# Gates and two projections of a hybrid decoder layer: weights as the moving operand, and a merged matrix turned by transposes

## The chip, the core and the metric

The kernel runs on one core of one Trainium2 chip. The metric is the device time of one execution in microseconds (us), the median of several runs. A core has a matrix engine (TensorE, PE), a vector engine (VectorE, DVE), a scalar engine (ScalarE, ACT), GpSimd (POOL), a sync engine (SyncE, SP) that here only issues transfers, and 16 DMA engines. Each engine works through its own instructions in order; semaphores connect them.

## The reference

One decoder layer over 256 tokens of width 2048, float32. Two mixers share one normalised input and one input projection; their outputs are projected, weighted by gates, added, projected again and added to the input:

```python
h = rms_norm(x, norm_w)
p = h @ w_in                                   # 2048 x 12416
(p_r, p_k, p_v, z_a, p_wd, p_ad, p_q, p_kq, p_vq, z_b, g_a, g_b) = split(p)
y_a = rwkv7_mix(p_r, p_k, p_v, p_wd, p_ad, ...) * silu(z_a)      # 16 heads of 64, recurrence
y_b = moba_attention(p_q, p_kq, p_vq, ...) * silu(z_b)           # 16 heads of 64, causal
merged = sigmoid(g_a) * (y_a @ w_proj_rwkv) + sigmoid(g_b) * (y_b @ w_proj_moba)
x = x + merged @ w_out
```

With 256 tokens the attention has one block, so it is plain causal attention. `g_a` and `g_b` are 2048 columns each; both projections go from 1024 to 2048 columns.

## The kernel before

**Three passes for one product.** Every large product is done in a reduced float32 format (fp32r) with both operands split into a high and a low part: hi x hi, lo x hi and hi x lo are added up in PSUM. The normalised input, turned so that channels lie in partitions, stands split in `xh` and `xl`. The row scale of the normalisation is not in them; it is applied to results, as `rbc` (tokens along columns) or `rsx` (tokens in partitions).

**Weights.** A chunk is 512 columns of a weight matrix. Its rows come in loads of 1 MB (`emit_load`, L235, two buffers `raw`), issued by SP. Each load makes two half-loads ("jobs" in the code) of 128 partitions x 1024 numbers: four blocks of 128 rows for a load, two for a half-load. ACT copies a half-load rounded into `hi` (L216), DVE subtracts to get `lo` (L222); three buffers each. A half-load is split two ahead of its use. There are 258 half-loads: 98 for the first seven projections of both head groups, 32 for the two SiLU gates, 64 for the sigmoid gates, 32 for the two projections, 32 for the output projection. In the rest of this text they are counted from 0.

**Two forms of the product.** `mm_fm` (L329) has 128 weight columns stationary and 256 tokens moving; the result has channels in partitions. One half-load is 2 row blocks x 4 column blocks x 3 = 24 passes of 256 columns. `mm_tm` (L347 to L349) has 128 tokens stationary and 512 weight columns moving; the result has tokens in partitions. One half-load is 2 row blocks x 2 token blocks x 3 = 12 passes of 512 columns. Before the change the attention's q, k and v and the output projection use `mm_tm`, all else `mm_fm`.

**Side work.** The recurrence (`rwkv_elem`, `rwkv_r`, `rwkv_mid`, `rwkv_v`, `group_norm`) and the attention (`moba`) are generators. After each half-load `pump` takes one step of the queue and one of each urgent generator. In `moba`, L831 makes logits, L842 to L845 mask them and take the maximum, L849 is the exp, L856 and L857 normalise, L863 and L865 turn the probabilities, L878 multiplies by v. `rwkv_v` and `group_norm` use L672, L679, L696, L699, L706, L734, L743, L750, L753.

**Gates and projections.** `gate_post` scales a gate chunk by `rbc` on DVE (`normed`, L170) into slots of old buffers and takes the sigmoid on ACT (L930). ACT keeps the tables of one set of functions at a time: sigmoid, exp and root lie in different sets, and a change shows as ACT_TABLE_LOAD. `pb_post` multiplies the attention's projection by its gate, `pa_post` the recurrence's, adds both, and splits the sum into `mgh` and `mgl`, the stationary operands of the output projection.

**Order.** For all but the first six half-loads the order within each engine is made by a scheduler, which runs a model of the engines over the whole program. So an edit at one place can move instructions that it doesn't touch.

Of the kernel before, what the change touches and what calls it, by code (L numbers as in the profile page):

```python
# [36 lines left out]
def tile_hybrid_block(ctx: ExitStack, tc: tile.TileContext, x, pv, wdu, wau,  # L37
# [23 lines left out]
    def PSS():  # L61
        return psd.tile([P, 512], F32, tag="ps", name=nm("ps"))
# [4 lines left out]
    def f32(ap):  # L67
        return ap.bitcast(F32)
# [100 lines left out]
    def normed(o, ps):  # L169
        dve.tensor_tensor(o.rearrange("p (f t) -> p f t", f=2), ps.rearrange("p (f t) -> p f t", f=2),  # L170
                          rbc2, ALU.mult)
# [68 lines left out]
    def chunk(wsrc, c0, w, kts, mm, post, pre=None, acc=None):  # L240
        nk = 2048 // w
        st = {}
        for b in range(kts // nk):
            ld = dict(spec=(wsrc, b * nk * P, nk, c0, w))
            loads.append(ld)
            for hf in range(2):
                jobs.append(dict(ld=len(loads) - 1, hf=hf, st=st, mm=mm, k0=b * nk + hf * nk // 2,
                                 nk=nk // 2, w=w, last=kts - 1, first=(b == 0 and hf == 0),
                                 end=(b == kts // nk - 1 and hf == 1), post=post, pre=pre))
# [84 lines left out]
    def mm_tm(sh, sl, cuts=((0, 0, 512), (1, 0, 512)), done=None):  # L334
        def f(jb):
            st, w, nk = jb["st"], jb["w"], jb["nk"]
            if jb["first"]:
                st["ps"] = [PSS() if i > 1 else PSM() for i in range(len(cuts))]
            hi = jb["hi"].rearrange("p (k c) -> p k c", k=nk)
            lo = jb["lo"].rearrange("p (k c) -> p k c", k=nk)  # L340
            order = [(i, q) for i in range(nk) for q in range(len(cuts))]
            for i, q in sorted(order, key=lambda e: e[1]) if jb is jobs[-1] else order:
                t, ca, cb = cuts[q]
                k = jb["k0"] + i
                o = st["ps"][q][:, 0:cb - ca]
                ts, cs, end = slice(t * P, (t + 1) * P), slice(ca, cb), k == jb["last"]
                pe.matmul(o, sh[:, k, ts], hi[:, i, cs], start=(k == 0), stop=False)  # L347
                pe.matmul(o, sh[:, k, ts], lo[:, i, cs], start=False, stop=False)  # L348
                pe.matmul(o, sl[:, k, ts], hi[:, i, cs], start=False, stop=end)  # L349
                if end and done:  # L350
                    done(o, t, ca, cb)
        return f

    fm_x = mm_fm(lambda k: xh[:, k, :], lambda k: xl[:, k, :])
    tm_x = mm_tm(xh, xl)

    R = [dict(), dict()]
    wa = C("wa", [P, S])
# [562 lines left out]
    def gate_post(key, i):  # L921
        def post(st):
            if not gates:
                for tag, n in (("LL0", 4), ("LL1", 4), ("X64", 2), ("UV", 4), ("a", 2)):
                    gt = T(tag, [P, n, 512])
                    gslots.extend(gt[:, u, :] for u in range(n))
            for j in range(2):
                gt = gslots.pop(0)
                normed(gt, st["ps"][j])
                act.activation(gt, gt, AF.Sigmoid)  # L930
                gates[key, 2 * i + j] = gt
        return post

    ysp = {}
# [30 lines left out]
            dve.tensor_tensor(lv, y, f32(hv), ALU.subtract)  # L965
            yield

    def fm_y(key):
        return mm_fm(lambda k: ysp[key, "h"][k // 4][:, k % 4, :],
                     lambda k: ysp[key, "l"][k // 4][:, k % 4, :])  # L970

    mrg = {}
# [9 lines left out]

    mh_t, ml_t = [], []

    def pa_post(i):
        def post(st):
            if not mh_t:
                mh_t.append(cp.tile([P, KT, S], F32R, tag="xh", name="mgh"))
                ml_t.append(cp.tile([P, KT, S], F32R, tag="xl", name="mgl"))
            mt = T(("cs", "kk")[i % 2], [P, 2, 512])  # L990
            for j in range(2):
                m = mt[:, j, :]
                dve.tensor_tensor(m, gates["a", 2 * i + j], st["ps"][j], ALU.mult)
                dve.tensor_tensor(m, m, mrg[i, j], ALU.add)
                f0 = 4 * i + 2 * j
                hv = mh_t[0][:, f0:f0 + 2, :].rearrange("p f t -> p (f t)")
                lv = ml_t[0][:, f0:f0 + 2, :].rearrange("p f t -> p (f t)")
                act.activation(hv, m, AF.Copy)
                dve.tensor_tensor(lv, m, f32(hv), ALU.subtract)
        return post  # L1000

    def out_pre(i, st_x):
# [14 lines left out]
        return done  # L1017

    def out_mm(cuts, done):
        return lambda jb: mm_tm(mh_t[0], ml_t[0], cuts, done)(jb)  # L1020

    def then(post, *gens):
        def f(st):
# [5 lines left out]
    def need(mark):  # L1029
        return lambda: drain(mark)  # L1030
# [28 lines left out]
        chunk(w_in, C_ZA + 512 * i, 512, KT, fm_x, post)  # L1059
    for ki, key in enumerate("ab"):  # L1060
        for i in range(4):
            chunk(w_in, (C_GA if key == "a" else C_GB) + 512 * i, 512, KT, fm_x,
                  with_need("v1", gate_post(key, i)))
    for i in range(4):
        chunk(w_pm, 512 * i, 512, 8, fm_y("b"), pb_post(i), pre=need("y"))
        chunk(w_pr, 512 * i, 512, 8, fm_y("a"), pa_post(i))
    for i in range(4):
        sx = {}
        cuts = ((0, 0, 512), (1, 0, 256), (1, 256, 512)) if i == 3 else ((0, 0, 512), (1, 0, 512))
# [46 lines left out]
```

## Time and profile before

| | |
|---|---|
| median of 3 runs | 831.94 us (830.06 to 832.64) |
| the profiled execution | 834.34 us |
| its span, first to last instruction | 832.6 us |
| PE, PE weight loads, DVE, ACT, POOL busy | 98%, 92%, 66%, 50%, 4% |
| moved by DMA | 145.78 MB, 175 GB/s |
| two sigmoid gates and both projections, without side work | 519.80 to 740.67 us |
| output projection | 740.67 us to the end |

PE is the engine to look at: at 98% there is little time in which it waits. Matmuls are pipelined, so the duration of one (0.28 us for 256 columns) is longer than the distance from its start to the next one's start; in the timeline the distance is what counts, and it is called the pitch or the pace below. The same holds, to a lesser degree, of ACT and DVE: a row that begins before the last one's end shows the overlap. A row with "x8" stands for eight instructions that follow each other; a small float32 matmul appears as two instructions.

### The profile page before, as it was taken

How to read it: one execution, taken by the hardware profiler on the slowest of the kernel's cores; microseconds unless marked ns; L12 is line 12 of the kernel's file. 1: busy time of each engine (PE TensorE's matmuls, PEld its weight loads, DVE VectorE, ACT ScalarE, POOL GpSimd, SP SyncE). 2: the span in 40 equal slices, each digit the busy share in tenths (PEclk: the TensorE clock that was granted, in tenths of full speed). 3: DMA queues.
4: the chain of work that ended last, by engine and by line, in shares of the span. 5: the costliest groups of instructions: out<-in, count | busy, mean ns of one | idle time of the engine just before them, and what ended most of it. 6: DMA issues, size and time to landing. Idle time of an engine off the chain costs nothing.

```text
span 832.6 us, 15909 instructions
## 1 busy us (share of the span) xinstructions
PE 819.9 (98%) x6770; PEld 764.4 (92%) x6770; DVE 551.9 (66%) x776; ACT 417.8 (50%) x565; POOL 29.9 (4%) x42
## 2 busy tenths in 40 slices
PE   8999999999999999999999999999999999999998
PEld 7999778899998888999999999999999999998887
DVE  5869958956569679649974588644445566665453
ACT  6785446444437784444444487444344444443332
POOL 5001100000000003000000000000000000000000
PEclk9999999999999999999999999999999999999999
DMA  8564554654434544655673424655555555556772
GB/s 305 181 201 152 180 166 160 202 177 153 136 119 131 174 146 137 210 140 178 203 228 106 149 66 143 224 189 172 198 194 169 195 193 166 199 182 202 248 232 97
DMA packets 83206, 145.78 MB, mean 175 GB/s; under 512 B 11568, under 2 KB 13872, under 8 KB 83136
## 3 DMA queue, kind: packets, MB, share of 16 engines
q1 hardware_dynamic: 71584, 138.55, 51.2%
q10 hardware_dynamic: 11520, 6.16, 2.8%
q8 instruction: 53, 0.87, 0.4%
q14 instruction: 17, 0.14, 0.0%
q0 software_dynamic: 32, 0.05, 0.0%
HBM read 141.61 MB, written 3.15 MB: 174 GB/s over the span
## 4 chain that ended last, share of the span: by engine, by line
PE 90%; DMA 3%; DVE 3%; ACT 2%; issue 1%; ACTq 0%; SPq 0%; DVEq 0%
PE pm L329 55%; PE pm L348 9%; PE pm L347 9%; PE pm L349 9%; PE ps L534 1%; PE ps L672 1%; PE ps L679 1%; DMA cs<-td 1%; DMA sg<-gd 1%; DVE lo L222 1%; DMA td<-kk 1%; PE ps L878 1%; DMA raw<-in_w_in_dram 1%; PE ps L696 1%; PE ps L831 1%
## 5 line engine op out<-in xcount | busy, mean ns | idle before, releaser
L222 DVE TENSOR_TENSOR lo<-raw,hi 128x1024 fp32r<-128x1024 f32 (+1 forms) x259 | 314.4, 1217 | 211.8 <-ACT hi L216 210.9
L216 ACT ACTIVATE hi<-raw 128x1024 fp32r<-128x1024 f32 (+1 forms) x259 | 272.4, 1055 | 343.9 <-PE pm L329 195.9
L329 PE MATMUL pm<-xh,hi 128*128 128x256 f32 x1168 | 329.0, 283 | 1.1 <-ACT xh L144 1.1
L329 PE MATMUL pm<-xh,lo 128*128 128x256 f32 x1168 | 325.4, 280 | 3.6 <-DVE lo L222 3.6
L329 PE MATMUL pm<-xl,hi 128*128 128x256 f32 x1168 | 326.1, 280 | 0.0
L329 PEld LDWEIGHTS pm<-xh,hi 128*128 128x128 f32 x1168 | 221.2, 190 | 4.5 <-ACT xh L144 1.5
L329 PEld LDWEIGHTS pm<-xh,lo 128*128 128x128 f32 x1168 | 219.8, 189 | 4.7 <-DVE lo L222 4.5
L329 PEld LDWEIGHTS pm<-xl,hi 128*128 128x128 f32 x1168 | 219.7, 189 | 0.5
L348 PE MATMUL pm<-lo,xh 128*128 128x512 f32 x192 | 76.5, 398 | 0.0
L349 PE MATMUL pm<-hi,xl 128*128 128x512 f32 x192 | 75.5, 393 | 0.0
L347 PE MATMUL pm<-hi,xh 128*128 128x512 f32 x192 | 72.6, 398 | 0.0
L348 PE MATMUL pm<-lo,mgh 128*128 128x512 f32 (+1 forms) x128 | 48.4, 378 | 0.0
L349 PE MATMUL pm<-hi,mgl 128*128 128x512 f32 (+1 forms) x128 | 48.1, 376 | 0.0
L347 PE MATMUL pm<-hi,mgh 128*128 128x512 f32 (+1 forms) x128 | 44.4, 378 | 0.0
L348 PEld LDWEIGHTS pm<-lo,xh 128*128 128x128 f32 x192 | 36.1, 188 | 8.0 <-DVE lo L222 0.8
L349 PEld LDWEIGHTS pm<-hi,xl 128*128 128x128 f32 x192 | 36.1, 188 | 7.3
L347 PEld LDWEIGHTS pm<-hi,xh 128*128 128x128 f32 x192 | 35.9, 188 | 7.5
L347 PEld LDWEIGHTS pm<-hi,mgh 128*128 128x128 f32 x128 | 24.1, 188 | 4.7
L349 PEld LDWEIGHTS pm<-hi,mgl 128*128 128x128 f32 x128 | 24.0, 188 | 4.7
L348 PEld LDWEIGHTS pm<-lo,mgh 128*128 128x128 f32 x128 | 24.1, 188 | 4.4
L566 DVE TENSOR_TENSOR tmp<-sg,kk 64x31 f32<-64x31 f32 (+15 forms) x62 | 20.5, 330 | 10.4 <-DMA sg<-gd 9.2
L329 PE MATMUL pm<-bk,hi 128*128 128x256 f32 x128 | 22.8, 281 | 0.0
(275 smaller groups left out, 983.5 us busy)
## 6 DMA issues: line engine op xcount, KB each, us to landing
raw<-in_w_in_dram SPq DMA_DIRECT2D x94, 1024.0 KB, 5.1
raw<-in_w_out_dram SPq DMA_DIRECT2D x16, 1024.0 KB, 5.4
raw<-in_w_proj_moba_dram SPq DMA_DIRECT2D x8, 1024.0 KB, 5.1
raw<-in_w_proj_rwkv_dram SPq DMA_DIRECT2D x8, 1024.0 KB, 5.1
raw<-in_w_in_dram SPq DMA_DIRECT2D x5, 512.0 KB, 6.1
k<-in_x_dram ACTq DMA_DIRECT2D x4, 256.0 KB, 4.0
r<-in_x_dram ACTq DMA_DIRECT2D x4, 256.0 KB, 4.2
k<-in_x_dram SPq DMA_DIRECT2D x2, 256.0 KB, 4.9
```

The costliest lines, as they stand in the source:

```text
L216: act.activation(job["hi"][:, c], job["src"][:, c], AF.Copy)
L222: dve.tensor_tensor(job["lo"][:, c], job["src"][:, c], f32(job["hi"][:, c]), ALU.subtract)
L329: pe.matmul(o, (hi, hi, lo)[ps][:, i, cs], (mh, ml, mh)[ps](k), start=(k == 0 and fi % 2 == 0 and ps == 0), stop=(k == jb["last"] and ps = ...
L347: pe.matmul(o, sh[:, k, ts], hi[:, i, cs], start=(k == 0), stop=False)
L348: pe.matmul(o, sh[:, k, ts], lo[:, i, cs], start=False, stop=False)
L349: pe.matmul(o, sl[:, k, ts], hi[:, i, cs], start=False, stop=end)
L534: pe.matmul(pss[p][:, c * P:(c + 1) * P], bk[sl, fi, c].rearrange("p a t -> p (a t)"), ar[sl, fi, c].rearrange("p a t -> p (a t)"), start= ...
L566: dve.tensor_tensor(tv, gcol.to_broadcast([64, nt, j + 1]), trow.to_broadcast([64, nt, j + 1]), ALU.mult)
L672: pe.matmul(ps[64 * p:64 * p + 64, c0 + 64 * fi:c0 + 64 * fi + 64], LL[p][:, fi, c, which, :], UV[:, c, p, fi, :], start=(fi == 0), stop=( ...
L679: pe.matmul(ps[sl, c0 + 64 * fi:c0 + 64 * fi + 64], ar[sl, fi, c, which, :], St[sl, fi, :], start=False, stop=True, skip_group_check=True)
L696: pe.matmul(ps[sl, cols], X64[sl, fi * 4 + c, :], Zs[sl, cols], start=True, stop=True)
L831: pe.matmul(pss[p][:, i * nk:(i + 1) * nk], q[rows, fi, 0:P] if u == 0 else q[rows, fi, P:S], k[rows, fi, 0:nk], start=True, stop=True)
```

## The change

Gates and both projections use `mm_tm` instead of `mm_fm`: tokens are stationary, 512 columns of weights move. `mm_tm` gets functions in place of tensors, so that the stationary operand can come from the pieces of `ysp`. Gate results have tokens in partitions, so the row scale is a number per partition, which the sigmoid's ACT instruction applies itself; the DVE scaling goes. The merged matrix too comes out with tokens in partitions, and the output projection needs channels there: `turn_m` turns it with 8 PE transposes for each 512 columns, and the split into `mgh` and `mgl` reads them from PSUM.

```diff
-                pe.matmul(o, sh[:, k, ts], hi[:, i, cs], start=(k == 0), stop=False)
-                pe.matmul(o, sh[:, k, ts], lo[:, i, cs], start=False, stop=False)
-                pe.matmul(o, sl[:, k, ts], hi[:, i, cs], start=False, stop=end)
+                pe.matmul(o, sh(k)[:, ts], hi[:, i, cs], start=(k == 0), stop=False)
+                pe.matmul(o, sh(k)[:, ts], lo[:, i, cs], start=False, stop=False)
+                pe.matmul(o, sl(k)[:, ts], hi[:, i, cs], start=False, stop=end)
...
-            for j in range(2):
+            for t in range(2):
                 gt = gslots.pop(0)
-                normed(gt, st["ps"][j])
-                act.activation(gt, gt, AF.Sigmoid)
-                gates[key, 2 * i + j] = gt
+                act.activation(gt, st["ps"][t], AF.Sigmoid, scale=rsx[:, t:t + 1])
+                gates[key, 2 * i + t] = gt
...
-    def fm_y(key):
-        return mm_fm(lambda k: ysp[key, "h"][k // 4][:, k % 4, :],
+    def tm_y(key):
+        return mm_tm(lambda k: ysp[key, "h"][k // 4][:, k % 4, :],
                      lambda k: ysp[key, "l"][k // 4][:, k % 4, :])
...
+    def turn_m(i, mt):
+
+        yield
+        for half in range(2):
+            f0 = 4 * i + 2 * half
+            ps = PSS()
+            for u in range(2):
+                c = (2 * half + u) * P
+                for t in range(2):
+                    pe.transpose(ps[:, u * S + t * P:u * S + (t + 1) * P], mt[:, t, c:c + P], ident)
+            hv = mh_t[0][:, f0:f0 + 2, :].rearrange("p f t -> p (f t)")
+            lv = ml_t[0][:, f0:f0 + 2, :].rearrange("p f t -> p (f t)")
+            act.activation(hv, ps, AF.Copy)
+            dve.tensor_tensor(lv, ps, f32(hv), ALU.subtract)
+        yield
...
-            for j in range(2):
-                m = mt[:, j, :]
-                dve.tensor_tensor(m, gates["a", 2 * i + j], st["ps"][j], ALU.mult)
-                dve.tensor_tensor(m, m, mrg[i, j], ALU.add)
-                f0 = 4 * i + 2 * j
-                hv = mh_t[0][:, f0:f0 + 2, :].rearrange("p f t -> p (f t)")
-                lv = ml_t[0][:, f0:f0 + 2, :].rearrange("p f t -> p (f t)")
-                act.activation(hv, m, AF.Copy)
-                dve.tensor_tensor(lv, m, f32(hv), ALU.subtract)
+            for t in range(2):
+                m = mt[:, t, :]
+                dve.tensor_tensor(m, gates["a", 2 * i + t], st["ps"][t], ALU.mult)
+                dve.tensor_tensor(m, m, mrg[i, t], ALU.add)
+            urgent.append(turn_m(i, mt))
...
-            chunk(w_in, (C_GA if key == "a" else C_GB) + 512 * i, 512, KT, fm_x,
+            chunk(w_in, (C_GA if key == "a" else C_GB) + 512 * i, 512, KT, tm_x,
                   with_need("v1", gate_post(key, i)))
...
-        chunk(w_pm, 512 * i, 512, 8, fm_y("b"), pb_post(i), pre=need("y"))
-        chunk(w_pr, 512 * i, 512, 8, fm_y("a"), pa_post(i))
+        chunk(w_pm, 512 * i, 512, 8, tm_y("b"), pb_post(i), pre=need("y"))
+        chunk(w_pr, 512 * i, 512, 8, tm_y("a"), pa_post(i))
```

On PE, where the gates begin (half-load 130), the order goes from passes of 256 columns to passes of 512; `pm` is the PSUM result, `hi` and `lo` the weights, and `L696` a matmul of the recurrence.

```order
 L329 MATMUL pm_4626<-xh,lo_4845 128x256
-L329 MATMUL pm_4986<-xh,hi_4884 128x256
-L329 MATMUL pm_4986<-xl,hi_4884 128x256
-L329 MATMUL pm_4986<-xh,lo_4886 128x256
-L329 MATMUL pm_4986<-xh,hi_4884 128x256
-L329 MATMUL pm_4986<-xl,hi_4884 128x256
+L347 MATMUL pm_4986<-hi_4884,xh 128x512
+L348 MATMUL pm_4986<-lo_4886,xh 128x512
+L349 MATMUL pm_4986<-hi_4884,xl 128x512
+L347 MATMUL pm_4987<-hi_4884,xh 128x512
+L348 MATMUL pm_4987<-lo_4886,xh 128x512
 L696 MATMUL ps_4912<-Zs_4872,X_9_122 64x64 x8
```

The five passes shown of before cover two blocks of 128 weight columns, the five of now two blocks of 128 tokens.

On ACT, in the attention's softmax of the second head group, before the change: `bk` is the exp of `sg`, `LL0` the slots of the first gates, `a` and `st` belong to `group_norm`. hi_737, hi_740 and hi_745 are the splits of half-loads 141, 142 and 143.

```order
L849 ACT_TABLE_LOAD
L849 ACTIVATE bk_718_5421,smx_723_5437<-sg_711_5405,mx_722_5434 128x128 x4
L930 ACT_TABLE_LOAD
L930 ACTIVATE LL0_713_5409<-LL0_713_5409 128x512 x2
L216 ACTIVATE hi_737_5511<-raw_700_5286 128x1024
L734 ACTIVATE a_710_5402<-a_710_5402 128x512
L849 ACT_TABLE_LOAD
L849 ACTIVATE bk_718_5421,smx_725_5446<-sg_711_5405,mx_724_5443 128x128 x4
L216 ACTIVATE hi_740_5541<-raw_726_5451 128x1024
L393 ACT_TABLE_LOAD
L393 ACTIVATE st_709_5399<-st_709_5399,epsg_89 128x8
L216 ACTIVATE hi_745_5590<-raw_726_5451 128x1024
```

The same place on ACT now, from the split of half-load 147 (hi_767) on; hi_770 is half-load 148, `pm_729` and `pm_730` are the second gate chunk. Ahead of the first row stand, from hi_763 (half-load 146) on: the two L699 copies, a table load with the two sigmoids of the first gate chunk, a table load with all eight exps of 128 columns, and the L734 square. Behind the last row stands hi_776 (half-load 149), and then hi_779 and hi_783.

```order
L216 ACTIVATE hi_767_5595<-raw_754_5506 128x1024
L929 ACT_TABLE_LOAD
L929 ACTIVATE LL0_713_5313<-pm_729_5359,rsx_129 128x512
L849 ACT_TABLE_LOAD
L849 ACTIVATE bk_718_5323,smx_734_5391<-cs_712_5310,mx_733_5388 128x256 x2
L929 ACT_TABLE_LOAD
L929 ACTIVATE LL0_713_5313<-pm_730_5360,rsx_129 128x512
L216 ACTIVATE hi_770_5624<-raw_762_5565 128x1024
L393 ACT_TABLE_LOAD
L393 ACTIVATE st_709_5303<-st_709_5303,epsg_89 128x8
L849 ACT_TABLE_LOAD
L849 ACTIVATE bk_718_5323,smx_736_5398<-cs_712_5310,mx_735_5395 128x256 x2
```

The first logits (L831) stood on PE at the beginning of half-load 138 and now stand in half-load 144 (hi_755), behind two passes and L696. In the rest of half-load 144 stand L672, L679 and the second L831; 145 to 148 are now without side work; in 149, behind two passes, stand L750 and L863. Before, half-loads 138 and 139 held the two logits, and 142 held L750 and L863. In 147 to 150 both first passes with hi now stand ahead of the first pass with lo.

On PE, one of the four groups of transposes (L993), in the projection: the second half-load after the merge that wrote `cs_933`.

```order
L347 MATMUL pm_937_6637<-hi_935_6633,vq_781_5681 128x512
L347 MATMUL pm_938_6638<-hi_935_6633,vq_781_5681 128x512
L993 MATMUL ps_939_6651<-ident_80,cs_933_6626 128x128
L993 MATMUL ps_940_6658<-ident_80,cs_933_6626 128x128
L993 MATMUL ps_939_6651<-ident_80,cs_933_6626 128x128 x3
L993 MATMUL ps_940_6658<-ident_80,cs_933_6626 128x128 x3
L348 MATMUL pm_937_6637<-lo_936_6635,vq_781_5681 128x512
L349 MATMUL pm_937_6637<-hi_935_6633,v_782_5682 128x512
```

Eight transposes stand between passes of the next chunk; nothing stood there before.

## Rows read from the trace of the kernel before

**Rows 1.** The page: busy share of PE, and its granted clock in 40 slices.

```profile
PE 819.9 (98%) x6770; PEld 764.4 (92%) x6770; DVE 551.9 (66%) x776; ACT 417.8 (50%) x565; POOL 29.9 (4%) x42
...
PEclk9999999999999999999999999999999999999999
```

**Rows 2.** What PE waited for: us in total, times, longest us.

```profile
PE pm L329 <- DVE lo L222: 3.6, 3, 1.7
...
PE ps L863 <- ACT oT L883: 0.6, 1, 0.6
```

**Rows 3.** The chain (start, us, what), and busy time in two stretches.

```profile
519.80 220.87 PE pm L329 x1866
...
519.80:740.67 220.87, 220.87 (x1868) 220.87 (x1868) 122.31 (x120) 93.20 (x98) 0.00 (x0) 1.00 0.58 189
745.00:795.00 50.00, 50.00 (x220) 41.03 (x219) 24.99 (x23) 19.09 (x18) 0.00 (x0) 1.00 0.68 221
```

**Rows 4.** PE's timeline (start, us, instruction): passes of 256 columns, the faster pace.

```profile
378.22 0.28 PE L329 MATMUL pm<-xh,hi 128*128 128x256 f32 x1
...
379.58 0.28 PE L329 MATMUL pm<-xh,hi 128*128 128x256 f32 x1
```

**Rows 5.** PE's timeline: first pass of the output projection, and of its last chunk.

```profile
740.51 0.40 PE L347 MATMUL pm<-hi,mgh 128*128 128x512 f32 x1
...
806.44 0.51 PE L347 MATMUL pm<-hi,mgh 128*128 128x512 f32 x2
```

**Rows 6.** PE's timeline: eight transposes between passes of 512 columns.

```profile
155.65 0.62 PE L347 MATMUL pm<-hi,xh 128*128 128x512 f32 x2
156.12 1.03 PE L777 MATMUL ps<-ident,qkn 128*128 128x128 f32 x8
156.91 0.48 PE L348 MATMUL pm<-lo,xh 128*128 128x512 f32 x1
157.22 0.39 PE L349 MATMUL pm<-hi,xl 128*128 128x512 f32 x1
```

**Rows 7.** PE's timeline: small matmuls of recurrence and attention.

```profile
476.69 0.68 PE L696 MATMUL ps<-Zs,X 64*64 64x64 f32 x16
477.30 1.16 PE L831 MATMUL ps<-kn,qn 64*128 64x128 f32 x8
```

**Rows 8.** ACT's timeline in the softmax of the second head group.

```profile
480.72 1.28 ACT L849 ACT_TABLE_LOAD   x1 [2.52 <-DVE mx L845]
...
484.97 1.15 ACT L930 ACTIVATE LL<-LL 128x512 f32<-128x512 f32 x2
486.03 1.04 ACT L216 ACTIVATE hi<-raw 128x1024 fp32r<-128x1024 f32 x1
486.98 0.61 ACT L734 ACTIVATE a<-a 128x512 f32<-128x512 f32 x1
487.61 1.28 ACT L849 ACT_TABLE_LOAD   x1
488.91 0.40 ACT L849 ACTIVATE bk<-sg,mx 128x128 f32<-128x128 f32 x1
...
490.47 1.04 ACT L216 ACTIVATE hi<-raw 128x1024 fp32r<-128x1024 f32 x1
...
495.39 0.51 ACT L849 ACTIVATE bk<-cs,mx 128x256 f32<-128x256 f32 x1
...
497.38 1.04 ACT L216 ACTIVATE hi<-raw 128x1024 fp32r<-128x1024 f32 x1
```

**Rows 9.** DVE's timeline: masks, a maximum, the products of `group_norm`, a lo split.

```profile
479.75 0.69 DVE L844 TENSOR_REDUCE mx<-sg 128x4 f32<-128x512 f32 x1
...
488.25 1.36 DVE L842 COPY_PREDICATED cs<-mq,ps 128x512 f32<-128x512 uint8 x2
...
493.97 1.71 DVE L743 TENSOR_TENSOR a<-a,st 64x256 f32<-64x256 f32 x4
...
495.72 1.23 DVE L222 TENSOR_TENSOR lo<-raw,hi 128x1024 fp32r<-128x1024 f32 x1
```

More of the change, by code (lines that the diff above doesn't have):

```diff
@@ L354, in tile_hybrid_block @@
     fm_x = mm_fm(lambda k: xh[:, k, :], lambda k: xl[:, k, :])
-    tm_x = mm_tm(xh, xl)
+    tm_x = mm_tm(lambda k: xh[:, k, :], lambda k: xl[:, k, :])
     R = [dict(), dict()]
@@ L1019, in out_mm @@
     def out_mm(cuts, done):
-        return lambda jb: mm_tm(mh_t[0], ml_t[0], cuts, done)(jb)
+        return lambda jb: mm_tm(lambda k: mh_t[0][:, k, :], lambda k: ml_t[0][:, k, :], cuts, done)(jb)
     def then(post, *gens):
```

## The prediction

> **What bounds the kernel now.** I read the page's busy shares and clock first, then who waits for whom on TensorE (PE), then the chain that ended last, then PE's timeline. PE is busy 98% of the span at a granted clock of full speed, that is 2.4 GHz, in every slice [rows 1]. Its waits add up to a few microseconds: 3.6 us for the low halves of split weights and 0.6 us for one copy of ScalarE (ACT) [rows 2]. So the end is PE's own work in order, and an edit is worth what it takes from PE, minus whatever makes PE wait. From 519.80 us the chain is one unbroken run of 1866 passes of 256 columns, 220.87 us long, up to the output projection; VectorE (DVE) is busy there 122 us and ACT 93 us [rows 3]. Nothing but PE matters in that stretch.
>
> I count in half-loads: a half-load is 128x1024 weights, split by ACT into hi and by DVE into lo, and it feeds 24 passes of 256 columns or 12 passes of 512. Gates and both projections are 64 + 32 = 96 half-loads, number 130 to 225 of the program. What is left of the two mixers when the gates begin, the last steps of the recurrence and the second group's attention, is woven into the first half-loads of the gates.
>
> **Part 1, the passes.** Now: 220.87 us / 1866 = 118.4 ns a pass, 24 x 118.4 = 2.84 us a half-load, over 1866 / 24 = 77.75 half-loads [rows 3]. New form: the output projection already runs it. From 740.51 to 806.44 us it does 24 half-loads, so 65.93 / 24 = 2.747 us each, 229 ns a pass [rows 5]. With 2.747 us the stretch takes 77.75 x 2.747 = 213.6 us: 7.3 us less. The other 18.25 half-loads stand among small matmuls, and there the old passes run at either of two paces: 118 ns as above, or 12 passes from 378.22 to 379.58 us, 113.3 ns [rows 4], with which a half-load is 2.72 us and the new form loses 0.03 us. Between 18.25 x 0.09 = +1.7 and -0.5 us I take +0.5. **Gain 7.8 us**, bounds 6.8 to 9.0. The gain is this small because the columns streamed are the same; only the excess over two halves of a pass goes.
>
> The Trainium skill speaks against this part: TensorE: Matmul & The Clock Gate, section Back-to-back issue gap, gives a gap of N/2.4 + 2.5 ns, hence 109.2 and 215.8 ns, and 24 x 109.2 - 12 x 215.8 saves 31 ns a half-load. By it the gain would be an estimated 3.0 us, less than the transposes of part 2 cost, and the sum below +6.0 in place of +1.2. This trace has 118.4 and 229 ns, so the measured paces decide.
>
> **Part 2, the transposes.** 32 of 128x128, four groups of 8, each two half-loads after its merge. Eight such transposes already stand between 512-column passes: from 155.65 to 157.22 us lie 8 transposes and 3 passes, 1.57 - 3 x 0.229 = 0.88 us for the 8 [rows 6]. **Cost 4 x 0.88 = 3.5 us**, bounds 3.2 (0.79 us from the first one's start to the next pass) and 4.2 (20% more, were they slower beside other buffers). They wait for the merge on DVE: four 128x512 operations of 0.6 to 0.7 us, 2.6 us, and two lo splits of 1.2 us that share the queue, 5.1 us, against two half-loads or 5.5 us on PE. The cover is thin, and gone it would cost under 1 us each time. The last group is turned in half-load 2 of the output projection, and its columns are wanted in half-load 6.
>
> **Costing nothing.** The gates lose 16 DVE scalings, since ACT now scales in the sigmoid; DVE is idle nearly half of that time [rows 3]. Merge and split keep their counts. Output, tail and loads stay. Before half-load 130 the order is the same.
>
> **Part 3, the order on ACT.** The order shows what the diff doesn't. The scheduler has put the attention's first softmax some six half-loads later, and the sigmoids of two gate chunks into it instead of one. ACT carries both that and the hi splits, in order. I put T = 0 where PE begins half-load 144 (hi_755), and walk ACT's rows with pitches from the trace (start to next start): hi split 0.95, table load 1.29, four exps of 128 columns 1.56, of 256 columns 1.99, two sigmoids 1.06, the L734 square 0.6 [rows 8], and a root of 8 numbers a partition at an estimated 0.2; on DVE two masks 1.3, a maximum 0.6, a lo split 1.2, four L743 products 1.7 [rows 9].
> - PE: two passes, 0.6 us of L696 and 1.1 us of L831 [rows 7]; the first logits are in PSUM at 2.4. With the rest of 144 and some 2.3 us of small matmuls in it, PE begins 145 at 7.1, 146 at 9.9, and wants 147, 148 and 149 at 12.6, 15.4 and 18.1.
> - DVE: masks 1.3, two maxima 1.2, one scaling 0.1: the first exp may begin to load its table at 5.1. By then ACT has split 146 and done the first chunk's sigmoids.
> - ACT: table 6.4, eight exps 9.6, square 10.2, split of 147 done 11.2: in time, and its lo at 13.1 just about.
> - ACT: table, sigmoid, table, two exps, table, sigmoid = 3 x 1.29 + 2 x 0.55 + 1.0 = 6.0; split of 148 from 17.2, done 18.2, lo done 19.4. PE wanted it at 15.4: it waits 2.8 for hi, issues two passes, waits 0.8 for lo, and ends 148 at 21.8.
> - ACT: table, root, table, two exps = 3.8; split of 149 done at 22.9. PE waits 1.2. Then the L750 transposes wait 0.4 for the L743 products, which DVE begins only after the last exp (21.9), and lo of 149 comes another 0.4 late, at 25.6.
>
> PE ends 149 at 27.9, and with no wait it were 22.4. **Stall 5.5 us.** From 150 on hi and lo are ready ahead. In the old order four splits start between 480.7 and 497.4 us, among the same kind of work on ACT, three of them shown [rows 8]; the new one has three in 17.8 us. Bounds: 0 if PE is as well covered there as now [rows 2], 9 if the lo splits and products queue worse than walked.
>
> **Sum.** -7.8 + 3.5 + 5.5 = **+1.2 us**. The profiled execution took 834.34 us, so 835.5; the median of the runs is 831.94, and on that 833.1. That is 0.14%, inside the 0.3% (2.5 us) that a measurement of this kernel can tell from no change.
>
> **Rivals.**
> - **The softmax costs nothing (faster).** For it: ACT's waits now leave PE 0.6 us of idle time through five table loads. Against it: the rows above put two more table loads and a second chunk's sigmoids between fewer splits. -7.8 + 3.5 = -4.3, so 827.6; it is told from no change when the stall stays under 1.8 us.
> - **The stall is longer (slower).** Each new wait of PE lets the hi buffers free later, so that splits and loads behind it start later; with the splits of 150 to 152 late too, at half-loads 150 to 154, the stall is 8 to 9 us: -7.8 + 3.5 + 8.5 = +4.2, so 836.1. It decides from a stall of 6.8 us. For it: DVE's queue, where an L856 waits in front of the products. Against it: the walk has hi of 150 at 23.9, wanted at 27.9. A fall of the granted clock to 1.2 GHz in that pause would add 2.7 us for each half-load run at it; the clock stayed full through the 1.7 us wait of now [rows 1, 2].
> - **Table loads cost twice as much (slower).** Were ACT held for as long again at each of the six loads between 5.1 and 22.9, the stall would be 6 x 1.29 = 7.7 us longer, +8.9, so 840.8. Against it: each load's next operation starts 1.29 us after it [rows 8]. The Trainium skill, ScalarE: Activation LUTs, section What ACT_TABLE_LOAD costs, states about 1283 ns for the load and about 1380 ns for a drain with it; the trace shows the first number and no drain.
> - **The wide passes are slower among the gates (slower).** At 238 ns, as slow as two of the old ones, part 1 is gone and the sum +9. Against it: 229 ns in the output projection [rows 5], where the core moves 221 GB/s against 189 here [rows 3]. The rule cited in part 1 belongs here; by it the time would be 837.9.
>
> **How the numbers follow.** Forecast, stall between 1.8 and 6.8: 0.56. No stall: 0.20. Longer stall, clock included: 0.20. Table loads 0.02, slow passes 0.02. The range takes in the no-stall case to its middle and the longer stall with a little more: 827.5 to 837. Faster by over 0.3%: 0.20; within: 0.56; slower: 0.24.
>
> **What would show it.** Part 1: half-loads of 2.75 us from the middle of the gates to the end, all at 229 ns. Part 2: eight L993 transposes in about 0.88 us, four times, PE not waiting ahead of them. Part 3: two or three new waits of PE for hi L216 and lo L222 within some 25 us, some 495 to 520 us into the span, the longest near 3 us, and ACT's row of table loads just ahead. If PE shows no wait there, the walk is wrong and the kernel is about 4 us faster; if waits go on past half-load 150, or the clock row drops, it is slower.

## The result, and the profile after

The changed kernel took 836.23 us (median of 5 runs, 834.48 to 838.26) against 832.16 us before: a ratio of **1.0053, 95% interval 1.0034 to 1.0072**. Measured again beside other kernels, with 12 runs of it and 35 of before, it was 1.0031 (1.0016 to 1.0046). So it is slower, by some 2.6 to 4.4 us: by the first comparison beyond the 0.3% that the prediction had set for "no change", by the second at that bound.

The profiled execution took 838.26 us, its span 836.5. The page's busy shares and clock row, which answer [rows 1]:

```profile
PE 819.8 (98%) x5650; PEld 711.8 (85%) x5650; DVE 541.9 (65%) x760; ACT 422.0 (50%) x567; POOL 29.5 (4%) x42
...
PEclk9999999999999999999999999999999999999999
```

PE has 1120 instructions fewer and is busy as long as before. The share alone would say that nothing happened. PE's waits answer [rows 2] (us in total, times, longest us):

```profile
PE pm L329 <- DVE lo L222: 3.4, 2, 2.5
PE pm L347 <- ACT hi L216: 3.0, 1, 3.0
...
PE pm L348 <- DVE lo L222: 1.5, 3, 0.7
```

The last two are new: in the rewritten half-loads PE waits 3.0 us for ACT's hi split and 1.5 us for DVE's lo.

To see where the time went I cut the end of the program at marks that both kernels have: the first L696 matmul of the second group's recurrence (in half-load 130, the gates' first, behind five of its passes), the first pass of the projections, the first of the output projection ([rows 5] for before) and the last pass. PE's timeline of before, from the first pass of half-load 130 on:

```profile
442.25 0.28 PE L329 MATMUL pm<-xh,hi 128*128 128x256 f32 x1
...
442.91 0.68 PE L696 MATMUL ps<-Zs,X 64*64 64x64 f32 x16
...
649.17 0.28 PE L329 MATMUL pm<-qn,hi 128*128 128x256 f32 x1
...
828.21 0.28 PE L349 MATMUL ps<-hi,mgl 128*128 128x256 f32 x1
```

And of the changed kernel:

```profile
444.02 0.39 PE L347 MATMUL pm<-hi,xh 128*128 128x512 f32 x1
...
445.26 0.68 PE L696 MATMUL ps<-Zs,X 64*64 64x64 f32 x16
...
652.07 0.64 PE L347 MATMUL pm<-hi,qn 128*128 128x512 f32 x2
...
743.75 0.62 PE L347 MATMUL pm<-hi,mgh 128*128 128x512 f32 x2
...
832.33 0.28 PE L349 MATMUL ps<-hi,mgl 128*128 128x256 f32 x1
```

From L696 on, the gates take 206.26 us before and 206.81 after. But the five passes ahead of that mark are old ones before (0.66 us) and new ones after (1.24 us), which do twice as much of the half-load. So across the two forms the gates must be counted from their first pass: 206.92 and 208.05 us. The projections take 91.34 and 91.68, the output 87.70 and 88.58. That is +1.13, +0.34 and +0.88: **+2.35 us**. The changed kernel was 1.77 us late already at the first pass of half-load 130, in code that the change doesn't touch; the last section comes back to that.

**The gates.** In their middle PE runs as forecast from [rows 5]. Two first passes of half-loads:

```profile
561.43 0.62 PE L347 MATMUL pm<-hi,xh 128*128 128x512 f32 x2
...
564.17 0.62 PE L347 MATMUL pm<-hi,xh 128*128 128x512 f32 x2
```

A half-load takes 2.74 to 2.75 us; before it took 24 x 117.8 ns = 2.83 there. The gain is real, and it is given back at the gates' head. PE's timeline at half-loads 147 to 149 (the last column is idle time and what ended it):

```profile
507.76 0.62 PE L347 MATMUL pm<-hi,xh 128*128 128x512 f32 x2
509.09 0.51 PE L348 MATMUL pm<-lo,xh 128*128 128x512 f32 x1 [0.70 <-DVE lo L222]
...
514.65 0.73 PE L347 MATMUL pm<-hi,xh 128*128 128x512 f32 x2 [2.98 <-ACT hi L216]
515.91 0.80 PE L348 MATMUL pm<-lo,xh 128*128 128x512 f32 x1 [0.52 <-DVE lo L222]
...
517.78 0.63 PE L347 MATMUL pm<-hi,xh 128*128 128x512 f32 x1
518.21 0.63 PE L348 MATMUL pm<-lo,xh 128*128 128x512 f32 x1
...
522.34 0.51 PE L348 MATMUL pm<-lo,xh 128*128 128x512 f32 x1 [0.26 <-DVE lo L222]
```

Between 515.91 and 519 us most passes take 0.43 us in place of 0.23. The busy time by stretches gives the granted clock in its third column from the end:

```profile
510.00:515.00 5.00, 2.02 (x10) 1.33 (x8) 1.23 (x3) 4.94 (x9) 0.00 (x0) 1.00 0.66 210
515.00:520.00 5.00, 4.48 (x13) 3.28 (x12) 2.37 (x6) 4.96 (x9) 0.00 (x0) 0.66 0.00 0
```

0.66 is a mean of full speed and of 1.2 GHz. The page's clock row shows a 9 there, because its slices are 21 us long. ACT's timeline of the same place, which answers [rows 8]; the three hi splits are those of 147, 148 and 149 with what follows it:

```profile
496.71 1.28 ACT L929 ACT_TABLE_LOAD   x1
500.01 1.27 ACT L929 ACTIVATE LL<-pm,rsx 128x512 f32<-128x512 f32 x2 [2.02 <-PE ps L672]
501.30 1.28 ACT L849 ACT_TABLE_LOAD   x1
...
506.21 1.04 ACT L216 ACTIVATE hi<-raw 128x1024 fp32r<-128x1024 f32 x1
507.27 1.28 ACT L929 ACT_TABLE_LOAD   x1
508.57 0.69 ACT L929 ACTIVATE LL<-pm,rsx 128x512 f32<-128x512 f32 x1
509.26 1.28 ACT L849 ACT_TABLE_LOAD   x1
...
511.67 1.28 ACT L929 ACT_TABLE_LOAD   x1
...
513.55 1.05 ACT L216 ACTIVATE hi<-raw 128x1024 fp32r<-128x1024 f32 x1
...
518.52 1.99 ACT L216 ACTIVATE hi<-raw 128x1024 fp32r<-128x1024 f32 x2
```

Between the splits of 146 and 149 ACT does twelve exps, two gate chunks' sigmoids and seven table loads. The first sigmoids, moreover, stand idle 2.02 us until the recurrence's L672 has read LL0 for the last time, since LL0 is their output slot; everything behind them on ACT waits too.

**The transposes** stand between passes, as in [rows 6]:

```profile
679.89 0.62 PE L347 MATMUL pm<-hi,vq 128*128 128x512 f32 x2
680.35 1.04 PE L993 MATMUL ps<-ident,cs 128*128 128x128 f32 x8
681.14 0.48 PE L348 MATMUL pm<-lo,vq 128*128 128x512 f32 x1
681.46 0.40 PE L349 MATMUL pm<-hi,v 128*128 128x512 f32 x1
```

From 679.89 to 681.46 are 1.57 us, as in [rows 6], and no row has a wait of PE ahead of L993.

### The profile page after: what moved, and what is told of

Its sections match the earlier page's. It is cut to its first block, busy times and chain, and to the rows that moved or that the text cites. A ratio compares the mean times of both kernels' runs of the same rounds, so it can differ in the third digit from the quotient of the medians.

```text
span 836.5 us, 13603 instructions
## 1 busy us (share of the span) xinstructions
PE 819.8 (98%) x5650; PEld 711.8 (85%) x5650; DVE 541.9 (65%) x760; ACT 422.0 (50%) x567; POOL 29.5 (4%) x42
## 4 chain that ended last, share of the span: by engine, by line
PE 92%; DMA 3%; ACT 2%; DVE 2%; issue 1%; ACTq 0%; POOL 0%; DVEq 0%; POOLq 0%
PE pm L329 25%; PE pm L348 19%; PE pm L347 19%; PE pm L349 19%; PE ps L534 1%; PE ps L672 1%; PE ps L679 1%; DMA sg<-gd 1%; DMA cs<-td 1%; PE ps L878 1%; PE ps L831 1%; DMA td<-kk 1%; PE ps L863 1%; PE ps L696 1%; ACT bk L849 1%
## 5 line engine op out<-in xcount | busy, mean ns | idle before, releaser
L216 ACT ACTIVATE hi<-raw 128x1024 fp32r<-128x1024 f32 (+1 forms) x259 | 272.0, 1055 | 340.2 <-PE pm L349 185.3
L329 PE MATMUL pm<-xh,lo 128*128 128x256 f32 x656 | 181.8, 280 | 3.4 <-DVE lo L222 3.4
L329 PE MATMUL pm<-xh,hi 128*128 128x256 f32 x656 | 184.4, 284 | 0.5 <-ACT xh L144 0.5
L329 PE MATMUL pm<-xl,hi 128*128 128x256 f32 x656 | 182.6, 280 | 1.0 <-DVE xl L149 1.0
L348 PE MATMUL pm<-lo,xh 128*128 128x512 f32 x448 | 178.8, 399 | 1.5 <-DVE lo L222 1.5
L349 PE MATMUL pm<-hi,xl 128*128 128x512 f32 x448 | 176.4, 394 | 0.0
L347 PE MATMUL pm<-hi,xh 128*128 128x512 f32 x448 | 166.2, 397 | 3.0 <-ACT hi L216 3.0
L329 PEld LDWEIGHTS pm<-xh,lo 128*128 128x128 f32 x656 | 123.9, 190 | 4.1 <-DVE lo L222 4.1
L329 PEld LDWEIGHTS pm<-xh,hi 128*128 128x128 f32 x656 | 123.2, 189 | 2.7 <-ACT xh L144 0.9
L329 PEld LDWEIGHTS pm<-xl,hi 128*128 128x128 f32 x656 | 123.5, 189 | 1.5 <-DVE xl L149 1.2
L347 PEld LDWEIGHTS pm<-hi,xh 128*128 128x128 f32 x448 | 84.1, 189 | 21.8 <-ACT hi L216 3.4
L348 PEld LDWEIGHTS pm<-lo,xh 128*128 128x128 f32 x448 | 84.7, 189 | 20.9 <-DVE lo L222 3.4
L347 PE MATMUL pm<-hi,mgh 128*128 128x512 f32 (+1 forms) x128 | 44.4, 377 | 0.0
L347 PEld LDWEIGHTS pm<-hi,mgh 128*128 128x128 f32 x128 | 24.0, 188 | 4.8
```

The costliest lines, as they stand in the source:

```text
L216: act.activation(job["hi"][:, c], job["src"][:, c], AF.Copy)
L329: pe.matmul(o, (hi, hi, lo)[ps][:, i, cs], (mh, ml, mh)[ps](k), start=(k == 0 and fi % 2 == 0 and ps == 0), stop=(k == jb["last"] and ps = ...
L347: pe.matmul(o, sh(k)[:, ts], hi[:, i, cs], start=(k == 0), stop=False)
L348: pe.matmul(o, sh(k)[:, ts], lo[:, i, cs], start=False, stop=False)
L349: pe.matmul(o, sl(k)[:, ts], hi[:, i, cs], start=False, stop=end)
```

## The experiments

Each edit shown is one to the changed kernel. All ratios are to the kernel before on the same chip, with 95% intervals. The stretches are those above, from each kernel's own profile. "From L696" is the one that the expectations mean; it compares kernels whose gates begin in the same form. "All gates" counts from the first pass of half-load 130, which adds 0.66 us where that half-load is in the old form and 1.24 us where it is in the new one; it compares any two. The stretches mostly repeat to within 0.1 us where nothing differs (206.26 and 206.25 with the old gates; 206.81, 206.82 and 206.78 with the new ones), which makes them a finer measure than the whole time. One does not: the kernel without transposes has the new gates too, and they take 207.33 there; why is not shown.

| kernel | ratio | gates, from L696 | all gates | projections | output |
|---|---|---|---|---|---|
| before | 1 | 206.26 | 206.92 | 91.34 | 87.70 |
| changed | 1.0053 (1.0034 to 1.0072) | 206.81 | 208.05 | 91.68 | 88.58 |
| gates alone | 1.0008 (0.9989 to 1.0027) | 206.78 | 208.03 | 91.44 | 87.70 |
| projections alone | 1.0031 (1.0013 to 1.0049) | 206.25 | 206.91 | 91.74 | 88.58 |
| no transposes | 0.9997 (0.9979 to 1.0016) | 207.33 | 208.57 | 88.99 | 87.72 |
| first two gate chunks old | 0.9981 (0.9965 to 0.9997) | 202.68 | 203.35 | 91.68 | 88.58 |
| changed, again | 1.0031 (1.0016 to 1.0046) | 206.82 | 208.05 | 91.67 | 88.58 |
| chunk 0 of all old | 0.9971 (0.9955 to 0.9986) | 202.66 | 203.32 | 91.52 | 88.58 |
| other slots | 0.9986 (0.9970 to 1.0001) | 201.97 | 203.22 | 91.67 | 88.58 |
| no sigmoid | 0.9982 (0.9967 to 0.9996) | 202.54 | 203.78 | 91.68 | 88.58 |
| late sigmoids | 0.9956 (0.9941 to 0.9971) | 200.52 | 201.76 | 91.67 | 88.58 |
| two steps | 1.0009 (0.9988 to 1.0030) | 205.34 | 206.58 | 91.67 | 88.58 |

### One part at a time

**Gates alone.**

```diff
-        chunk(w_pm, 512 * i, 512, 8, tm_y("b"), pb_post(i), pre=need("y"))
-        chunk(w_pr, 512 * i, 512, 8, tm_y("a"), pa_post(i))
+        chunk(w_pm, 512 * i, 512, 8, fm_y("b"), pb_post(i), pre=need("y"))
+        chunk(w_pr, 512 * i, 512, 8, fm_y("a"), pa_post(i))
...
```

> Only the gates with tokens in rows; both projections and the merge stay as before, with no transposes, so the gates' two halves stand in another layout than the projections they multiply, and the output is not the reference's. Theory 1 (the order on ACT: PE stalls about 7 us between half-loads 144 and 149, and the passes save 4.8 us of the 7.8): about 832 - 4.8 + 7.4 = 834.7 us, with the same PE waits for hi and lo and the same fall of the granted clock after them as the changed kernel. Theory 2 (the time came with the projections and their transposes): about 827.5 us, and no such waits.

831.52 us against 831.39. The mechanism came as expected, the size did not: the wait is there (`pm L347 <- hi L216`, us in total, times, longest),

```profile
PE pm L347 <- ACT hi L216: 3.0, 1, 3.0
```

and the granted clock is 0.66 from 510 to 520 us; but the gates are 1.1 us longer than before, not 2.6, since their passes gain 5.3 us, not 4.8, and the stall is 6.5 us, not 7.4 (both worked out below). Theory 2 fell: the stall is the gates' own.

**Projections alone.**

```diff
-            chunk(w_in, (C_GA if key == "a" else C_GB) + 512 * i, 512, KT, tm_x,
+            chunk(w_in, (C_GA if key == "a" else C_GB) + 512 * i, 512, KT, fm_x,
...
```

> Only the two projections with tokens in rows, with the 32 transposes; the gates stay as before, so layouts don't match and the output is not the reference's. Theory 1: 32 half-loads x 0.094 = -3.0 us, transposes +3.5, no new wait: about 832.6 us. Theory 2: most of the 4 us by which the changed kernel is slower appear here: about 836 us, with waits at L993 or in the half-loads around it.

833.9 us, +2.5 against 831.4 (interval 1.1 to 4.1). The stretches give +0.40 and +0.88, so +1.3, and PE has no wait at L993 or in the half-loads beside it. Theory 1's +0.5 was somewhat low, theory 2's 836 much too high.

**No transposes.**

```diff
-            urgent.append(turn_m(i, mt))
...
+                hv = mh_t[0][:, f0:f0 + 2, :].rearrange("p f t -> p (f t)")
...
+                act.activation(hv, m, AF.Copy)
+                dve.tensor_tensor(lv, m, f32(hv), ALU.subtract)
```

> The changed kernel without the 32 transposes: the merged matrix is split as it stands (tokens in rows), so the output is not the reference's. Theory 1: the transposes cost their 4 x 0.88 = 3.5 us and nothing else: 836.2 - 3.5 = 832.7 us. A rival in which the transposes are hidden under the passes' loads: 836 us; one in which PE also waits around them: under 831 us.

831.54 us, a ratio 0.0034 or 2.8 us below the changed kernel's in the second comparison. The stretches are finer: projections 91.68 - 88.99 = 2.69 us for three groups, output 88.58 - 87.72 = 0.86 for the fourth. Nothing hides them, and nothing waits around them. The 0.5 us by which this kernel's own gates are longer hides part of that gain in the whole time.

The second comparison of the changed kernel ran beside the next three:

> The changed kernel once more, unaltered, beside the next three on one chip, since the two parts measured alone (gates 1.0008, projections 1.0031 of the kernel before) add up to less than the 1.0053 first measured. Theory 1 (the parts are independent): about 1.003 to 1.004 of the kernel before; the profile splits into gates +0.5 us, projections with transposes +0.4, the fourth group of transposes in the output projection +0.9. Rival (the two parts together cost something that neither has alone): 1.005 or more, with a stretch in the profile that neither of the two alone shows.

834.74 us against 832.21, with stretches equal to the first profile's. So the parts do add up: +1.1 us from the gates, +1.2 to 1.3 from the projections, transposes and output.

### Is it the order at the gates' head?

**The first two gate chunks old.** Half-loads 130 to 145 in the old form put ACT's work back in the order of before, with the softmax some half-loads earlier.

```diff
-            chunk(w_in, (C_GA if key == "a" else C_GB) + 512 * i, 512, KT, tm_x,
+            chunk(w_in, (C_GA if key == "a" else C_GB) + 512 * i, 512, KT, fm_x if key == "a" and i < 2 else tm_x,
...
```

> The changed kernel with the first two gate chunks (half-loads 130 to 145) in the old form, the other six and the projections in the new; those two chunks are in the wrong layout, so the output is not the reference's. The order of ACT around half-loads 140 to 150 is that of before again. Theory 1 (the stall comes from the moved softmax and recurrence, not from the new passes): 80 half-loads x 0.094 = -7.5, transposes +3.5, no stall: about 828.1 us and PE's waits as before. Rival (the new passes or the two sigmoids a chunk on ACT are slower whatever the order): 834 to 836 us, with waits of PE for hi at the first new chunk.

830.41 us, 0.9981. The gates fall by 4.7 us to 203.35, and PE waits as before. The rival, new passes slow in any order, fell. The total is above the 828.1 that I expected: the 48 new half-loads of the gates gained 0.074 us each (3.57 in all), not 0.094, and the projections with their transposes lost 1.2 us, not 0.5.

**Chunk 0 of gates and projections old**, a complete kernel with the same order (the old sigmoid and split that chunk 0 needs are not shown):

```diff
-    for ki, key in enumerate("ab"):
-        for i in range(4):
-            chunk(..., tm_x, with_need("v1", gate_post(key, i)))
+    for i in range(4):
+        for key in "ab":
+            chunk(..., tm_x if i else fm_x, with_need("v1", gate_post(key, i)))
...
```

> A complete kernel: chunk 0 of both gates, run first, and chunk 0 of both projections stay in the old form (with the merge split directly), the other three of each in the new one, with 24 transposes. ACT has the order of before around half-loads 140 to 150. Theory 1 (the stall is a matter of the order at the head of the gates): gates -3.6 us as measured with the first two chunks old, projections 3/4 of -2.0 = -1.5, transposes 3 x 0.89 = +2.7: -2.4 us, ratio about 0.997, the gates' stretch at 202.7 us. Rival (the gain of the gates hangs on something else than the order): ratio 1.000 or more, gates' stretch 204 us or longer.

829.69 us, 0.9971, gates' stretch 202.66: as expected, and faster than the kernel before and the changed one.

### What in the order costs it?

**Other slots.** One line: the first chunk's sigmoids write to X64, which the recurrence is done with earlier. The scheduler's order changes with it.

```diff
-                for tag, n in (("LL0", 4), ("LL1", 4), ("X64", 2), ("UV", 4), ("a", 2)):
+                for tag, n in (("X64", 2), ("LL0", 4), ("LL1", 4), ("UV", 4), ("a", 2)):
```

> The changed kernel with one edit: the first gate chunk's sigmoids write to the two slots of X64, which the recurrence reads last some steps before LL0. In the changed kernel they wait 2.0 us on ACT for the recurrence's last read of LL0, with all later work of ACT behind them; here the order also puts both sigmoids of the second chunk together, with one pair of table loads (2.6 us) less. Theory 1 (ACT's queue is what PE waits for): split 148 ends some 6 us earlier, before PE wants it; one wait of 1 to 2 us for split 149 is left, the granted clock stays full, and the time is 4 to 5 us below the changed kernel. Rival (PE waits for the late softmax itself, not for splits behind it): the waits move to the logits and products, and less than 2 us is saved.

The stretch is 201.97, 4.85 us less than the changed kernel's. ACT's timeline, with the table load of the first exps and splits 147 and 148:

```profile
500.52 1.28 ACT L849 ACT_TABLE_LOAD   x1 [0.81 <-DVE mx L845]
...
505.44 1.05 ACT L216 ACTIVATE hi<-raw 128x1024 fp32r<-128x1024 f32 x1
506.50 1.28 ACT L929 ACT_TABLE_LOAD   x1
507.79 1.26 ACT L929 ACTIVATE LL<-pm,rsx 128x512 f32<-128x512 f32 x2
508.95 1.05 ACT L216 ACTIVATE hi<-raw 128x1024 fp32r<-128x1024 f32 x1
```

Split 148 follows 147 by 3.5 us, where it followed by 7.3. The slot's own wait is the smaller part of that gain. Counted from the last L696 (495.62 us here, 495.19 in the changed kernel), the exps' table load starts 1.2 us earlier, no more, since it now waits for DVE's maximum; split 147 comes 1.2 us earlier, split 148 5.0. The other 3.8 us are the order: a pair of table loads fewer, and two exps that went behind split 148. No run changes the slot and keeps the order. The wait for 148 is gone, the clock stays full here, and two waits of 0.9 us are left on PE, not the one of 1 to 2 us for split 149 that I had expected:

```profile
509.73 0.51 PE L348 MATMUL pm<-lo,xh 128*128 128x512 f32 x1 [0.91 <-DVE lo L222]
...
515.99 0.63 PE L750 MATMUL ps<-ident,a 128*128 128x128 f32 x4 [0.93 <-DVE a L743]
```

The whole time is only 3.6 us below the changed kernel's (831.11 against 834.74); the profile of this kernel, too, lost time ahead of the gates.

**No sigmoid.**

```diff
-                act.activation(gt, st["ps"][t], AF.Sigmoid, scale=rsx[:, t:t + 1])
+                act.activation(gt, st["ps"][t], AF.Identity, scale=rsx[:, t:t + 1])
```

> The changed kernel with the gates' sigmoid left out (scaling alone, on ACT, as many operations of the same size), so no table load for it; the output is not the reference's. The order is the changed kernel's, the wait of 2.0 us for LL0 stays. Theory 1: split 147 as late as in the changed kernel, split 148 about 4 us earlier, so PE's wait of 3.0 us at 148 goes, and a wait of 2 to 2.5 us at 149 comes in its place; about 3 us saved. Rival (table loads are not the cost; the LL0 wait and the softmax alone decide): less than 1 us saved and the wait at 148 stays.

Stretch 202.54, 4.3 us less. The wait for 148 is gone and one for 149 has come, 0.95 us where I had put 2 to 2.5:

```profile
506.37 0.50 PE L348 MATMUL pm<-lo,xh 128*128 128x512 f32 x1 [0.71 <-DVE lo L222]
...
512.64 0.73 PE L347 MATMUL pm<-hi,xh 128*128 128x512 f32 x2 [0.95 <-ACT hi L216]
```

The sigmoids' wait for LL0 on ACT is still there, 3.3 us long, and the stretch is 2.0 us above that of the next kernel, where it is gone; how much of that it costs is not shown. So the table loads taken away alone bring 148 in time. The slot wait alone was never taken away: an estimate from the 1.2 us above leaves PE 1.8 of the 2.98 us at 148.

**Late sigmoids**, a complete kernel: DVE scales the first two chunks out of PSUM, and their sigmoids are tied to the third chunk's result.

```diff
-                act.activation(gt, st["ps"][t], AF.Sigmoid, scale=rsx[:, t:t + 1])
+                late = key == "a" and i < 2
+                if late:
+                    dve.tensor_scalar(gt, st["ps"][t], rsx[:, t:t + 1], None, ALU.mult)
+                else:
+                    act.activation(gt, st["ps"][t], AF.Sigmoid, scale=rsx[:, t:t + 1])
...
+            if key == "a" and i == 2:
+                zl = T("zl", [P, 1])
+                dve.tensor_scalar(zl, st["ps"][1][:, 0:1], 0.0, None, ALU.mult)
+                for j in range(4):
+                    act.activation(gates["a", j], gates["a", j], AF.Sigmoid, bias=zl)
```

> A complete kernel: the changed kernel, but the first two gate chunks are scaled out of PSUM by DVE into their slots, and their sigmoids run in place on ACT only once the third chunk's result is there (a zero bias taken from it ties them to it). Neither chunk's sigmoid, nor its table loads, nor the wait for LL0 stands on ACT between the splits of half-loads 146 and 150 any more. Theory 1 (PE's stall is the splits' place behind sigmoids and tables on ACT): no wait of PE for hi in half-loads 147 to 149, at most 1.5 us for lo and L750, full clock, the gates' stretch at 200.5 to 202 us against 206.8, ratio to the kernel before about 0.995 to 0.996. Rival (the recurrence and the softmax, which stay late, cost the time themselves): the stretch at 204 us or more.

828.91 us against 832.53, 0.9956: the fastest of all. Splits 147, 148 and 149 come 2.4 us apart,

```profile
501.25 1.04 ACT L216 ACTIVATE hi<-raw 128x1024 fp32r<-128x1024 f32 x1
...
503.69 1.04 ACT L216 ACTIVATE hi<-raw 128x1024 fp32r<-128x1024 f32 x1
...
506.08 1.04 ACT L216 ACTIVATE hi<-raw 128x1024 fp32r<-128x1024 f32 x1
```

and PE's only wait between 470 and 530 us is one for a lo split:

```profile
508.74 0.50 PE L348 MATMUL pm<-lo,xh 128*128 128x512 f32 x1 [0.75 <-DVE lo L222]
```

The recurrence is as late here as in the changed kernel: its last L696 comes 49.93 us after the first in both, and 33.78 before. So the rival, that the lateness itself costs the time, fell: what cost was the place of the splits behind it.

**Two steps** in all chunks, as before the change:

```diff
-                act.activation(gt, st["ps"][t], AF.Sigmoid, scale=rsx[:, t:t + 1])
+                dve.tensor_scalar(gt, st["ps"][t], rsx[:, t:t + 1], None, ALU.mult)
+                act.activation(gt, gt, AF.Sigmoid)
```

> A complete kernel: the changed kernel with gate results taken as before in two steps, DVE scaling out of PSUM, then the sigmoid in place on ACT, in all eight chunks. The order on ACT now has split 148 right behind split 147, but a sigmoid with its table pair still ahead of split 149, and a sigmoid, a root and their tables ahead of split 150. Theory 1: the waits move to half-loads 149 and 150, 3 to 4 us in all, the gates' stretch at 204 to 205.5 us, ratio 0.999 to 1.001. Rival (freeing the accumulators by ACT, and not the order, made the stall): no waits for hi, the stretch under 202 us.

Stretch 205.34, 1.0009, as theory 1 had it, but with one wait for hi, at 149, one for L750, and three short ones for lo (1.3 us in all, not shown):

```profile
515.19 0.73 PE L347 MATMUL pm<-hi,xh 128*128 128x512 f32 x2 [1.67 <-ACT hi L216]
516.75 0.63 PE L750 MATMUL ps<-ident,a 128*128 128x128 f32 x4 [0.83 <-DVE a L743]
```

Which engine empties the accumulators is not the point; what stands ahead of a split is.

## Why the prediction was right or wrong

The forecast was 833.1 us, no change within 0.3%. The time came out 3.1 us above it in the first comparison, inside the range but past the 0.3%, and by the second at the very bound of it. Each part was there, at the place named.

- **Part 1, right in sum.** Without its one wait the late-sigmoid kernel's gates take 201.76 - 0.75 = 201.01 us, those of before without theirs 206.92 - 0.57 = 206.35 [rows 2]: 5.3 us gained. The projections without transposes gain 91.34 - 88.99 = 2.35. Together 7.7 us; 7.8 was forecast, 6.8 to 9.0 the bounds. That the sum fits so well is luck, as two errors cancel. The first 16 half-loads, where I took +0.5 us (for 18), gave 1.8 (201.01 against 203.35 - 0.57 = 202.78 in the kernel whose first two chunks are old); what gave it there is not shown, since the old passes among the small matmuls run partly at 113 to 114 ns (from 440 to 470 us). And a half-load of the plain rest of the gates gave 3.57 / 48 = 0.074 us, not 0.094, as the old passes there ran at 117.8 ns, not at the chain's mean of 118.4. The rule on the gap between matmuls in the Trainium skill (TensorE: Matmul & The Clock Gate, Back-to-back issue gap), which that section calls the gap of a single matmul by itself and by which an estimated 3.0 us would come, is not borne out: 117.8 and 228.9 ns here.
- **Part 2, right.** 2.69 + 0.86 = 3.55 us for four groups; 3.5 was forecast, and PE waits at none.
- **Part 3, right in place and mechanism, a little short.** The gates of the changed kernel are 208.05 - 201.01 = 7.0 us above those without waits; 0.57 was there before, so the stall costs 6.5 us against 5.5 forecast. Of the 7.0 us PE's four waits shown above are 4.5 and the low clock 1.6; the other 0.9 is not placed. The walk had 2.8 us of waiting for split 148; it was 2.98, with some luck, since the split ended 1.8 us later than walked and PE came to it 1.5 us later. Two terms failed. The walk let the first sigmoids run while ACT had nothing else to do, and overlooked that their slot LL0 was still being read: split 147 ended 1.4 us later than walked, 1.2 of it by the slot (compare the kernel with other slots), and PE waited 0.70 us for its lo. And it left the clock full. Eight passes from 515.91 us took 3.45 us in place of 1.83, 1.6 us more. In return the wait of 1.2 us forecast for split 149 did not come: PE, slowed, needed it later.
- **The clock was put in the wrong case.** I argued from one wait of 1.7 us at full clock that a fall belonged only to a stall of 8 us or more. Nothing in the trace of before bore on a pause of 3 us; I should have given the fall to the forecast's own 2.8 us wait as an even chance.
- **The sum.** Gates -5.3 + 6.5, projections -2.35 + 2.69, output +0.88: +2.35 us, each term unrounded, where +1.2 was forecast. The second comparison, +2.6 us (1.3 to 3.8), holds that; the first, +4.4 (2.8 to 6.0), does not quite. In the nine other kernels the interval of the ratio holds what the stretches sum to, in that of the other slots only just (-2.5 us, and the runs -2.5 to +0.1). In the kernels with new projections the medians lie 0 to 1.7 us above their sums, never below. What that is stays open.
- **The rivals.** No stall: what the late-sigmoid kernel then did, 828.9 us, where 827.6 was put for the whole. The longer stall, from 6.8 us on, was missed by 0.3 us by its own price, though its clock fall came. Table loads twice as dear: no. From 507.27 to 508.57 us one takes 1.30; the drain that the Trainium skill names (ScalarE: Activation LUTs, What ACT_TABLE_LOAD costs) does not show. Slow wide passes: no, 229 ns.

## What to carry to other kernels

A rewrite that speeds up the bounding engine's passes also makes a scheduler place the side work anew; walk the feeding engine's order through the few places where it changed, with every output slot's last reader, before counting the gain. When a feeder falls behind by a sum of small things (a slot wait, table switches), a cheap edit at one of them can restore most of the gain: here one swap in a list of slots, with the order that the scheduler then made, took 4.85 us off the gates, and moving two chunks' sigmoids out of the way 6.3. Read the new order before naming the cause, since such an edit seldom changes one thing only. A pause of the bounding engine may cost more than its length, because the clock may fall after it.

## What the runs showed that I had not expected

**The clock after a pause.** In all four profiles with the 3.0 us wait at split 148 (the changed kernel twice, gates alone, no transposes) the granted clock fell to 1.2 GHz for some passes after it, 0.43 us each; the wait of 1.67 us in the two-step kernel left it full. The same happens in code that the change doesn't touch. At about 374 us PE waits for a lo split, in the twelve profiles between 0.76 and 2.49 us. In the two longest the clock fell, here in the changed kernel:

```profile
374.33 0.39 PE L329 MATMUL pm<-xh,lo 128*128 128x256 f32 x1 [2.49 <-DVE lo L222]
...
376.42 0.41 PE L329 MATMUL pm<-xh,lo 128*128 128x256 f32 x1
376.63 0.41 PE L329 MATMUL pm<-xh,hi 128*128 128x256 f32 x1
```

In the kernel with other slots it fell after 2.02 us. It stayed full in the other ten, the longest of them this:

```profile
373.52 0.38 PE L329 MATMUL pm<-xh,lo 128*128 128x256 f32 x1 [1.95 <-DVE lo L222]
```

**Two paces at one clock.** In those two profiles the passes of 256 columns from 400 to 420 us run at 117.8 ns, in the other ten at 113.3, all at full granted clock. That and the fall are more than the 1.77 us by which the profile of the changed kernel was late ahead of its gates: the fall cost some 1.7 us, and some 490 passes from 380 us on, at 117.2 ns on the mean in place of 113.5, some 1.8; against them stands a wait of 0.9 us at 382 us that only before has. In the gates before, the pace is 117.8 ns from 520 us on; at 113.3 the old form (2.72 us a half-load) would beat the new one (2.75). What sets the pace is not settled. The projections, too, run slower than the gates in either form, 118.9 ns (91.34 us for 768 passes) and, without transposes, 231.7 (88.99 us for 384) against 117.8 and 228.9, at full clock and without waits; no run here says why.
